# Splitting weights with an accumulating DMA, and value parts side by side in banded attention

## The chip, the cores and the metric

One core of a Trainium2 chip runs the whole program. The metric is device time in microseconds (us) for one execution; lower is better. TensorE (PE) multiplies, VectorE (DVE), ScalarE (ACT) and GpSimd (POOL) do the elementwise work, SyncE (SP) and POOL issue DMAs.

## The reference

A two-layer decoder for 512 tokens, model width 1024, all in float32. Layer 0 is differential attention (8 heads, each with two 64-wide score parts and a 128-wide value) and a SwiGLU FFN of hidden width 2816. Layer 1 is banded attention (16 query heads, 4 key/value heads, head width 64, a window of 128 tokens, one learned sink per head) and another FFN.

```python
def diff_attention(...):                       # per block of 128 queries
    s = einsum('bqhcd,bkhcd->bhcqk', qblk, k) * scale
    p = softmax(where(causal, s, NEG_INF))
    a = p[:, :, 0] - lam * p[:, :, 1]
    o = rms_norm(einsum('bhqk,bkhe->bqhe', a, v), subln) * (1.0 - lambda_init)
    return o.reshape(B, S, DA_V) @ w_o

def swa_sink_attention(...):                   # keys: own block and the one before
    e = exp(s - m)
    p = e / (sum(e) + exp(sink - m))
    o = einsum('bnhgqk,bnkhd->bnqhgd', p, vw)
    return o.reshape(B, S, SW_HEADS * HEAD_DIM) @ w_o
```

## The kernel before

**Numbers in two parts.** PE multiplies in a rounded float32 format. To keep float32 accuracy each operand x is held as hi, x rounded by a cast on ACT, and lo = x - hi, made by a subtract on DVE. A product is three matmuls into one PSUM tile, hi·hi, hi·lo and lo·hi (`mm3`, L291 to L294).

**Weights.** `load_w` (L283) loads one unit (128 partitions x 1024 floats, 512 KB) with a DMA on SP into a tile tagged `raw`, of which two exist (`RAWB`), and `parts` (L262) splits it in two halves h = 0 and 1 of 128x512: the cast of L268, the subtract of L269. The tags `hi` and `lo` have 8 buffers each (`HLB`), four units. Where a norm's gain goes into the weights (L271 to L277, q/k/v of the banded layer) the cast and the subtract take the gain as a factor. `qk_units` loads four units and `v_units` two per pair of heads of the differential attention; `o_units` (L448) loads four for half of an output projection, for rows j = 0, 2 and column halves n = 0, 1, in the order (0,0), (0,1), (2,0), (2,1). `o_block` (L453) then goes, for one block of 128 tokens, through n = 0 with j = 0 to 3 and through n = 1 with j = 0 to 3, each j a `mm3`. The FFN's own splitter (L583 to L587) already has a `move` form: ACT writes the negated rounded value into lo, a DMA issued by POOL adds raw to it in place, and ACT casts hi.

**Stages.** In time: differential attention to about 270 us, its FFN to 600, banded attention to about 785, its FFN to the end. The differential attention runs its four pairs of heads one after the other; the q/k/v products of the next pair, and for the last pair the output projection `o_da`, fill PE between the steps of the current one. `o_da(0, ..)` covers the first two pairs (rows 0 to 511 of the output weights), `o_da(1, ..)` the last two; its first token block runs at 244 to 252 us.

**Banded attention.** It has 16 work units, one per key/value head and query block. Each takes `score` (PE scores, DVE mask and maximum, ACT exponential at L1399 and scaling by the reciprocal sum at L1406), `turn_p` (PE transposes the weights at L1418, ACT and DVE split them into ph and pl of 128x512, four heads of 128 queries side by side) once per key block, and `weigh` (L1424). Query block 0 has one key block, the others two. `weigh` forms the output of four heads in a 128x256 PSUM tile `po`, one buffer: heads 0 and 2 of a group on partitions 0 to 63 and heads 1 and 3 on 64 to 127. For that it keeps v in `vpad`, 64 columns of v with zeros on either side, and shifts the window by 64 columns for e = 0 and 1: two e, three matmuls of 128x256 each, per key block. `split_evac` then reads `po` twice, the cast to `oh` on ACT and the subtract to `ol` on DVE.

**Order.** PE's order is the order of the program text: the tables `DA_STEPS`, `DA_STEPS3`, `SW_AT` give each step a slot, and `Fill` puts so much of the filling products between two slots. DVE, ACT, POOL and SP are ordered by the framework's scheduler, by priorities (`boost` for weight splitting, `evac`, `HOT`). Each engine runs its list in order and waits where an operand or a buffer isn't ready.

## Time and profile before

| | us |
|---|---|
| timed runs | 1122.22, 1124.5, 1125.8 (median 1124.5) |
| profiled execution, span | 1121.8 |
| PE busy | 1101.6 (98%) |
| DVE busy | 1008.4 (90%) |
| ACT busy | 711.3 (63%) |
| POOL busy | 55.5 (5%) |
| median from issue to landing, accumulating DMA of 256 KB | 3.8 |

The profile is one execution, taken by the hardware profiler. Each row of its views has a line of the kernel, an engine, the operation, and output<-inputs by the program's names. What an engine is busy is not what it costs: a wait counts where it holds up work on the engine that sets the end. The time of a profiled execution is its span; the timed runs are separate executions.

### The profile page before, as it was taken

The page shows a single profiled execution, that of the slowest core. Times are in us where ns is not written, and L with a number is a line of the kernel's source. Part 1 is how long each engine was busy: PE and PEld are TensorE (multiplying, and loading weights), DVE is VectorE, ACT ScalarE, POOL GpSimd, SP SyncE. Part 2 cuts the span into 40 slices and gives each one's busy share as a digit, 9 for nine tenths or more (in the row PEclk, how much of TensorE's full clock was granted, in tenths as well). Part 3 has the DMA queues.
Part 4 walks back from the last instruction along what each step waited for, and adds up shares of the span by engine and source line. Part 5 has one row for each costly group of instructions (what it writes and reads, how often), then busy time and mean ns, then how long its engine had stood idle before and what let it go on. Part 6 is the DMA issues. An engine that isn't in the chain of part 4 may idle for free.

```text
span 1121.8 us, 20162 instructions
## 1 busy us (share of the span) xinstructions
PE 1101.6 (98%) x7206; PEld 978.3 (87%) x7206; DVE 1008.4 (90%) x2418; ACT 711.3 (63%) x1577; POOL 55.5 (5%) x76
## 2 busy tenths in 40 slices
PE   8999999999999999999999999999999999999998
PEld 6878888778989989989998778878989989998997
DVE  5979798979999899999998787988899999899997
ACT  6575756454555665675678499697555666566574
POOL 1100000000000010010003000000010000000000
PEclk9999999999999999999999999999999999999999
DMA  6312121124453434336124311120545247246213
GB/s 198 113 57 77 38 77 50 65 72 140 146 162 98 141 80 160 112 82 203 57 48 106 111 41 57 39 76 25 198 138 168 76 104 207 85 104 178 77 30 103
DMA packets 94085, 114.90 MB, mean 102 GB/s; under 512 B 5993, under 2 KB 70914, under 8 KB 93986
## 3 DMA queue, kind: packets, MB, share of 16 engines
q1 hardware_dynamic: 87216, 100.97, 28.1%
q0 software_dynamic: 6720, 12.65, 6.3%
q8 instruction: 56, 0.92, 0.3%
q14 instruction: 43, 0.35, 0.1%
q10 hardware_dynamic: 50, 0.01, 0.0%
HBM read 99.98 MB, written 2.10 MB: 91 GB/s over the span
## 4 chain that ended last, share of the span: by engine, by line
PE 77%; DVE 12%; ACT 6%; DMA 2%; issue 1%; SPq 1%; DVEq 0%; ACTq 0%
PE acc L721 16%; PE tr L721 10%; PE tr L809 9%; PE acc L809 8%; PE acc L292 8%; PE acc L294 8%; PE acc L293 8%; PE po L721 2%; PE tr L435 2%; ACT s L1399 2%; DVE hss L385 1%; ACT s L1406 1%; DVE lo L587 1%; DMA r<-in_w_gate_up_dram 1%; PE tr L310 1%
## 5 line engine op out<-in xcount | busy, mean ns | idle before, releaser
L585 ACT CAST hi<-r 128x512 fp32r<-128x512 f32 x160 | 98.9, 620 | 79.5 <-PE acc L721 35.8
L292 PE MATMUL acc<-hi,hTh 128*128 128x512 f32 (+1 forms) x352 | 132.9, 377 | 2.5 <-DVE vl L1022 1.4
L293 PE MATMUL acc<-lo,hTh 128*128 128x512 f32 (+1 forms) x352 | 124.1, 353 | 0.4 <-DVE lo L269 0.4
L294 PE MATMUL acc<-hi,hTl 128*128 128x512 f32 (+1 forms) x352 | 124.2, 353 | 0.1
L585 ACT CAST hi<-g 128x512 fp32r<-128x512 f32 x154 | 94.9, 618 | 40.8 <-PE acc L293 19.2
L587 DVE TENSOR_TENSOR lo<-r,hi 128x512 fp32r<-128x512 f32 x160 | 105.3, 692 | 6.1 <-ACT hi L585 5.8
L585 ACT CAST hi<-raw 128x512 fp32r<-128x512 f32 x108 | 66.9, 621 | 62.5 <-PE tr L721 18.2
L792 ACT CAST ah<-lf 128x256 fp32r<-128x256 f32 x154 | 61.1, 404 | 47.9 <-PE tr L809 16.0
L721 PE MATMUL acc<-hTh,lo 128*128 128x256 f32 x288 | 81.6, 283 | 0.0
L721 PE MATMUL acc<-hTl,hi 128*128 128x256 f32 x288 | 81.5, 283 | 0.0
L721 PE MATMUL acc<-hTh,hi 128*128 128x256 f32 x288 | 81.5, 283 | 0.0
L721 PE MATMUL acc<-tl,hi 128*128 128x256 f32 x288 | 81.2, 282 | 0.0
L721 PE MATMUL acc<-th,hi 128*128 128x256 f32 x288 | 81.1, 282 | 0.0
L721 PE MATMUL acc<-th,lo 128*128 128x256 f32 x288 | 81.1, 282 | 0.0
L268 ACT CAST hi<-raw 128x512 fp32r<-128x512 f32 x96 | 57.3, 619 | 33.9 <-PE acc L294 24.6
L292 PEld LDWEIGHTS acc<-hi,hTh 128*128 128x128 f32 x352 | 66.7, 190 | 13.4 <-issue 2.6
L587 DVE TENSOR_TENSOR lo<-g,hi 128x512 fp32r<-128x512 f32 x110 | 76.1, 692 | 1.5 <-ACT hi L585 1.4
L294 PEld LDWEIGHTS acc<-hi,hTl 128*128 128x128 f32 x352 | 66.5, 189 | 10.1 <-DVE hTl L907 0.7
L584 POOL DMA_DIRECT2D lo<-g x44 | 38.5, 976 | 716.4 <-ACT lo L583 372.3
L587 DVE TENSOR_TENSOR lo<-raw,hi 128x512 fp32r<-128x512 f32 x108 | 73.4, 692 | 0.0
L269 DVE TENSOR_TENSOR lo<-raw,hi 128x512 fp32r<-128x512 f32 x96 | 64.7, 688 | 9.4 <-ACT hi L268 8.9
L293 PEld LDWEIGHTS acc<-lo,hTh 128*128 128x128 f32 x352 | 66.9, 190 | 6.5 <-DVE lo L269 0.7
(280 smaller groups left out, 3644.7 us busy)
## 6 DMA issues: line engine op xcount, KB each, us to landing
r<-in_w_gate_up_dram SPq DMA_DIRECT2D x80, 512.0 KB, 5.0
g<-in_w_down_dram SPq DMA_DIRECT2D x88, 256.0 KB, 5.4
lo<-g POOLq DMA_DIRECT2D x44, 256.0 KB, 3.8
raw<-in_da_w_qkv_dram SPq DMA_DIRECT2D x30, 256.0 KB, 3.3
raw<-in_da_w_qkv_dram SPq DMA_DIRECT2D x8, 512.0 KB, 3.7
raw<-in_da_w_o_dram SPq DMA_DIRECT2D x8, 512.0 KB, 3.7
raw<-in_w_gate_up_dram SPq DMA_DIRECT2D x8, 512.0 KB, 3.7
raw<-in_sw_w_o_dram SPq DMA_DIRECT2D x8, 512.0 KB, 3.8
```

What stands on the lines that cost most here:

```text
L268: nc.scalar.copy(hi, part)
L269: nc.vector.tensor_tensor(lo, part, hi.bitcast(F32), op=ALU.subtract)
L292: nc.tensor.matmul(dst, sh, mh, start=start, stop=False)
L293: nc.tensor.matmul(dst, sh, ml, start=False, stop=False)
L294: nc.tensor.matmul(dst, sl, mh, start=False, stop=stop)
L435: nc.tensor.matmul(banks[c][:, cols], q[a][rows], k[b][rows], start=a + b == 0, stop=a == 1)
L584: nc.gpsimd.dma_start(out=lo.bitcast(F32), in_=src, accum_op=ALU.add)
L585: nc.scalar.copy(hi, src)
L587: nc.vector.tensor_tensor(lo, src, hi.bitcast(F32), op=ALU.subtract)
L721: nc.tensor.matmul(dst, l[:, k, :], r[:, k, :], start=fresh and k == 0 and i == 0, stop=k == 3 and i == 2, skip_group_check=not fresh)
L792: nc.scalar.copy(ah, src)
L809: nc.tensor.matmul(bank, l[:, tk], r, start=fresh and i == 0 and n == 0, stop=i == len(qs) - 1 and n == 2, skip_group_check=not fresh)
```

## The change

**Moved halves.** `parts` gets a form `move` for the second half (h = 1) of unscaled weights: ACT writes lo = -raw (rounded), a DMA issued by POOL adds raw to it in place, and ACT casts hi. The subtract on DVE goes. Since lo is raw minus raw's rounded value, the numbers are the same. It is used in `qk_units` of pairs 1 to 3 (12 halves), `v_units` of pairs 1 to 3 (6), and the two `o_units` of each attention (16): 34 halves. POOL's list grows from 73 to 107 rows. Pair 0's v, its hand-written first units, the banded layer's scaled q/k/v weights and the FFN's weights are split as before.

**Value parts side by side.** `vpad` and its zeroing go. `vv` holds vh and vl of one head as 128 adjacent columns. Per key block `weigh` now has two matmuls of 128x512, [vh|vl] with ph and with pl, so partitions 0 to 63 of `po` get vh·(ph+pl) and 64 to 127 vl·(ph+pl), for all four heads. ACT copies the lower half of `po` to `ocor` (64x512), DVE adds the halves in two adds of 64x256 into `osum` in SBUF, one of them onto partitions 64 to 127, and `split_evac` splits `osum`. PE has 56 matmuls there in place of 168.

```diff
@@ -259,12 +259,16 @@
             hi, lo = self.halves[i // self.n]
             return hi[:, i % self.n, :], lo[:, i % self.n, :]
 
-    def parts(unit, raw, h, gains=None, by_cols=False):
+    def parts(unit, raw, h, gains=None, by_cols=False, move=False):
         a, b = raw.shape[1:]
         part = raw[:, :, h * b // 2:(h + 1) * b // 2] if by_cols else raw[:, h * a // 2:(h + 1) * a // 2, :]
         hi = wp.tile(list(part.shape), F32R, name=nm("hi"), tag="hi", bufs=HLB)
         lo = wp.tile(list(part.shape), F32R, name=nm("lo"), tag="lo", bufs=HLB)
-        if gains is None:
+        if move:
+            nc.scalar.activation(lo, part, AF.Copy, scale=-1.0)
+            nc.gpsimd.dma_start(out=lo.bitcast(F32), in_=part, accum_op=ALU.add)
+            nc.scalar.copy(hi, part)
+        elif gains is None:
             nc.scalar.copy(hi, part)
             nc.vector.tensor_tensor(lo, part, hi.bitcast(F32), op=ALU.subtract)
         else:
@@ -277,7 +281,7 @@
                                                    op0=ALU.mult, op1=ALU.subtract)
         unit.halves.append((hi, lo))
 
-    def load_w(srcs, a, b, gains=None, by_cols=False):
+    def load_w(srcs, a, b, gains=None, by_cols=False, moved=()):
         unit = Split(a, b, by_cols)
         with tc.high_priority(offset=pri["boost"]):
             raw = wp.tile([P, a, b], F32, name=nm("raw"), tag="raw", bufs=RAWB)
@@ -285,7 +289,7 @@
             for i, src in enumerate(srcs):
                 nc.sync.dma_start(out=raw[:, :, i * w:(i + 1) * w], in_=src)
             for h in range(2):
-                parts(unit, raw, h, gains, by_cols)
+                parts(unit, raw, h, gains, by_cols, h in moved)
         return unit
 
     def mm3(dst, sh, sl, mh, ml, start, stop):
@@ -447,7 +451,7 @@
 
     def o_units(w, k0):
         wv = w.rearrange("(k p) n -> p k n", p=P)
-        return {(j, n): load_w([wv[:, k0 + j:k0 + j + 2, n * 512:(n + 1) * 512]], 2, 512)
+        return {(j, n): load_w([wv[:, k0 + j:k0 + j + 2, n * 512:(n + 1) * 512]], 2, 512, moved=(1,))
                 for j in (0, 2) for n in range(2)}
 
     def o_block(units, pieces, t, ready=None):
@@ -996,11 +1000,12 @@
         def qk_units(self):
             units = []
             for k in range(0, KT, 2):
-                units.append(load_w([wq3[:, k:k + 2, s, self.cs] for s in range(2)], 2, 512))
+                units.append(load_w([wq3[:, k:k + 2, s, self.cs] for s in range(2)], 2, 512, moved=(1,)))
             return units
 
         def v_units(self):
-            return [load_w([wq3[:, k:k + 4, 2, self.cs]], 4, 256) for k in range(0, KT, 4)]
+            moved = (1,) if self.p else ()
+            return [load_w([wq3[:, k:k + 4, 2, self.cs]], 4, 256, moved=moved) for k in range(0, KT, 4)]
 
         def qk_post(self, pts):
             self.ts = copy_out(self.ap, pts, 512)
@@ -1278,7 +1283,7 @@
         ap.tile([P, D], F32, name="s", tag="s", bufs=4)
         ap.tile([P, 512], F32, name="t", tag="t", bufs=4)
         maskS = maskD[:, 256:512]
-        vpad = [ap.tile([P, NT, 9, HD], F32R, name=nm("vpad"), tag=f"vpad{e}") for e in range(2)]
+        vv = ap.tile([P, NT, 4, 2, HD], F32R, name=nm("vv"), tag="vv")
         kT = new_kT(ap, "kTs")
         wqv = sw_w_q[0].rearrange("(k p) n -> p k n", p=P)
         wkv = w_kv.rearrange("(k p) n -> p k n", p=P)
@@ -1290,8 +1295,6 @@
             nc.gpsimd.dma_start(out=gsw[:, 1, :], in_=k_norm.partition_broadcast(P))
             nc.gpsimd.affine_select(out=maskS[:, 0:P], in_=maskS[:, 0:P], pattern=[[1, P]],
                                     compare_op=ALU.is_gt, fill=NEG, base=0, channel_multiplier=-1)
-            for e in range(2):
-                nc.gpsimd.memset(vpad[e][:, :, 0::2, :].bitcast(F32), 0.0)
             tables(Cs, Ss, gsw, HD, nc.gpsimd, nc.gpsimd)
 
         def units_of(*parts):
@@ -1337,10 +1340,10 @@
                     nc.scalar.copy(tt, pts[t][:, 0:256])
                 ts["B"].append(tt)
                 src = heads(pts[t][:, 256:512])
-                dh = vpad[0][:, t, 1::2, :]
+                dh = vv[:, t, :, 0, :]
                 with tc.high_priority(offset=HOT):
                     nc.scalar.activation(dh, src, AF.Copy, scale=rx[:, t:t + 1])
-                    nc.vector.scalar_tensor_tensor(vpad[1][:, t, 1::2, :], src, rx[:, t:t + 1], dh.bitcast(F32),
+                    nc.vector.scalar_tensor_tensor(vv[:, t, :, 1, :], src, rx[:, t:t + 1], dh.bitcast(F32),
                                                    op0=ALU.mult, op1=ALU.subtract)
             vdone.add(0)
             scl["B"] = head_stats(ap, ts["B"], 4)
@@ -1427,15 +1430,19 @@
             po = att("po")
             assert vdone
             for b, blk in enumerate(blocks):
-                for e in range(2):
-                    c0 = (2 * kv + 1 - e) * HD
-                    vf = [vpad[z][:, blk].rearrange("p a e -> p (a e)")[:, c0:c0 + P] for z in range(2)]
-                    es = slice(e * 256, (e + 1) * 256)
-                    mm3(po[:, 0:256], vf[0], vf[1], pT[u, b][0][:, es], pT[u, b][1][:, es],
-                        b == 0 and e == 0, b == nb - 1 and e == 1)
+                v = vv[:, blk, kv].rearrange("p z e -> p (z e)")
+                for z in range(2):
+                    nc.tensor.matmul(po, v, pT[u, b][z], start=b == 0 and z == 0, stop=b == nb - 1 and z == 1)
             oh = ap.tile([P, 2, P], F32R, name=nm("oh"), tag="oh", bufs=OSW)
             ol = ap.tile([P, 2, P], F32R, name=nm("ol"), tag="ol", bufs=OSW)
-            split_evac(oh, ol, po[:, 0:256].rearrange("p (h q) -> p h q", q=P))
+            osum = ap.tile([P, 256], F32, name=nm("osum"), tag="osum", bufs=2)
+            ocor = ap.tile([P, 512], F32, name=nm("ocor"), tag="ocor", bufs=2)
+            with tc.high_priority(offset=pri["evac"]):
+                nc.scalar.copy(ocor[0:HD, :], po[HD:P, :])
+                for e in range(2):
+                    es = slice(e * 256, (e + 1) * 256)
+                    nc.vector.tensor_tensor(osum[e * HD:(e + 1) * HD, :], po[0:HD, es], ocor[0:HD, es], op=ALU.add)
+            split_evac(oh, ol, osum.rearrange("p (h q) -> p h q", q=P))
             o_all[kv, i] = (oh, ol)
 
         def pieces_sw(ch):
```

**Where the order moves: ACT at the end of the differential attention.** ACT's list near the last two units of the output projection's second half; before (raw_659 is unit (0,1), raw_664 is (2,0), raw_669 is (2,1), aT are the transposed weights of the last pair, osb its evacuated output):

```order
L268 CAST hi_665_3197<-raw_664_3195 128x512
L268 CAST hi_667_3201<-raw_664_3195 128x512
L298 CAST aT_644_3102<-tr_647_3105 128x128
L298 CAST aT_635_3076<-tr_650_3130 128x2x128
L298 CAST aT_644_3102<-tr_649_3118 128x2x128
L298 CAST aT_636_3077<-tr_650_3130 128x2x128
L1121 COPY osb_652_3170<-po_651_3145 128x512
L1123 ACTIVATE osq_653_3172<-osb_652_3170 128x512
L268 CAST hi_670_3207<-raw_669_3205 128x512
L268 CAST hi_672_3211<-raw_669_3205 128x512
```

And of the changed kernel, from the last aT on, with the line numbers of its own text (L268 is the negating cast, L270 the hi cast of a moved half, L272 that of an unmoved one; raw_659, raw_664 and raw_669 are the same units):

```order
L302 CAST aT_636_3099<-tr_650_3152 128x2x128
L272 CAST hi_665_3221<-raw_664_3219 128x512
L270 CAST hi_667_3225<-raw_664_3219 128x512
L268 ACTIVATE lo_663_3215<-raw_659_3208 128x512
L268 ACTIVATE lo_668_3226<-raw_664_3219 128x512
L1126 COPY osb_652_3192<-po_651_3167 128x512
L1128 ACTIVATE osq_653_3194<-osb_652_3192 128x512
L272 CAST hi_670_3232<-raw_669_3230 128x512
L270 CAST hi_672_3236<-raw_669_3230 128x512
L268 ACTIVATE lo_673_3237<-raw_669_3230 128x512
L526 ACTIVATE xn_689_3331,fss_688_3330<-xs_76 128x1024
```

Both casts of (2,0) have moved behind the last aT; the negating casts of (0,1) and (2,0) come after them, and that of (2,1) after both of its hi casts.

**ACT in the middle of the banded attention.** From a split of the weights (ph) to the scaling by the reciprocal sum of the next work unit; s_1856 before and s_1871 after are the same unit's weights. Before:

```order
L298 CAST ph_1867_9344<-tr_1866_9339 128x512
L268 CAST hi_1896_9449<-raw_1893_9443 128x512
L1399 ACTIVATE s_1856_9285,sm_1860_9305<-s_1856_9285,mx_1857_9286,hscl_1758_8875 128x256 x4
L1401 ACTIVATE es_1861_9308<-es_1861_9308 128x4
L298 CAST oh_1878_9397<-po_1877_9390 128x256
L298 CAST q_1883_9410<-tr_1882_9407 128x256
L298 CAST ph_1886_9422<-tr_1885_9417 128x512
L1406 ACTIVATE s_1856_9285<-s_1856_9285,rs_1862_9316 128x256 x4
```

And now (raw_1912 is unit (0,1) of the second output half, raw_1917 is (2,0)):

```order
L302 CAST ph_1884_9356<-tr_1883_9351 128x512
L270 CAST hi_1910_9452<-raw_1907_9446 128x512
L302 CAST oh_1879_9336<-osum_1881_9338 128x256
L272 CAST hi_1913_9459<-raw_1912_9457 128x512
L270 CAST hi_1915_9463<-raw_1912_9457 128x512
L1441 COPY ocor_1898_9408<-po_1894_9402 64x512
L1402 ACTIVATE s_1871_9296,sm_1875_9316<-s_1871_9296,mx_1872_9297,hscl_1767_8891 128x256 x4
L1404 ACTIVATE es_1876_9319<-es_1876_9319 128x4
L302 CAST oh_1895_9405<-osum_1897_9407 128x256
L268 ACTIVATE lo_1916_9464<-raw_1912_9457 128x512
L272 CAST hi_1918_9470<-raw_1917_9468 128x512
L1409 ACTIVATE s_1871_9296<-s_1871_9296,rs_1877_9327 128x256 x4
```

A copy ocor, a negating cast and the first cast of (2,0) now stand ahead of the scaling (L1409), and the q and ph casts have moved behind it.

**PE at one value product.** One work unit with two key blocks, and what follows. Before:

```order
L292 MATMUL po_1961_9707<-ph_1930_9581,vpad_1487_7623 128x256
L293 MATMUL po_1961_9707<-pl_1931_9582,vpad_1487_7623 128x256
L294 MATMUL po_1961_9707<-ph_1930_9581,vpad_1488_7624 128x256
L292 MATMUL po_1961_9707<-ph_1930_9581,vpad_1487_7623 128x256
L293 MATMUL po_1961_9707<-pl_1931_9582,vpad_1487_7623 128x256
L294 MATMUL po_1961_9707<-ph_1930_9581,vpad_1488_7624 128x256
L292 MATMUL po_1961_9707<-ph_1936_9610,vpad_1487_7623 128x256
L293 MATMUL po_1961_9707<-pl_1937_9611,vpad_1487_7623 128x256
L294 MATMUL po_1961_9707<-ph_1936_9610,vpad_1488_7624 128x256
L292 MATMUL po_1961_9707<-ph_1936_9610,vpad_1487_7623 128x256
L293 MATMUL po_1961_9707<-pl_1937_9611,vpad_1487_7623 128x256
L294 MATMUL po_1961_9707<-ph_1936_9610,vpad_1488_7624 128x256
```

And now:

```order
L1435 MATMUL po_1984_9718<-ph_1951_9595,vv_1487_7649 128x512
L1435 MATMUL po_1984_9718<-pl_1952_9596,vv_1487_7649 128x512
L1435 MATMUL po_1984_9718<-ph_1959_9621,vv_1487_7649 128x512
L1435 MATMUL po_1984_9718<-pl_1960_9622,vv_1487_7649 128x512
L1421 MATMUL tr_1989_9732<-ident_80,s_1936_9523 128x128 x4
```

Twelve matmuls of 128x256 have become four of 128x512; the transposes of the next unit's weights follow as before.

## The prediction

> **What bounds the kernel now.** I read the page's totals and chain first, then a table of busy time by stage, then the waits of PE, and last the timelines of the two places where a moved half is wanted soon. The page, its first part and its chain:
>
> ```profile
> span 1121.8 us, 20162 instructions
> PE 1101.6 (98%) x7206; PEld 978.3 (87%) x7206; DVE 1008.4 (90%) x2418; ACT 711.3 (63%) x1577; POOL 55.5 (5%) x76
> PE 77%; DVE 12%; ACT 6%; DMA 2%; issue 1%; SPq 1%; DVEq 0%; ACTq 0%
> ```
>
> PE is the bound on average, but PE runs in an order written out by hand, so what it waits for at one place counts at once. The table by stage (window: length, then busy us and instructions of PE, PEld, DVE, ACT and POOL); the first row is the end of the differential attention, the others are the banded attention:
>
> ```profile
> 212.00:262.00 50.00, 47.52 (x258) 37.92 (x257) 40.26 (x129) 23.74 (x57) 0.29 (x1) 1.00 0.14 43
> 645.00:700.00 55.00, 52.30 (x329) 41.84 (x328) 43.43 (x173) 49.76 (x144) 0.00 (x0) 1.00 0.16 50
> 728.00:760.00 32.00, 31.59 (x207) 25.22 (x206) 26.43 (x97) 29.02 (x81) 0.00 (x0) 1.00 0.22 67
> 760.00:786.00 26.00, 25.00 (x155) 20.81 (x153) 22.87 (x69) 20.61 (x50) 0.00 (x0) 1.00 0.13 37
> ```
>
> ACT, 63% over the span, is at 90% in the first and second banded rows (49.76 of 55, 29.02 of 32). Work added to ACT there isn't free. Both FFN stages run their old code, so I give them 0. PE's waits in the end of the differential attention (us in total, times, longest):
>
> ```profile
> PE po L1140 <- DVE ro L249: 1.3, 2, 1.0
> PE tr L1100 <- DVE s L1084: 1.2, 1, 1.2
> PE tr L435 <- DVE qkT L445: 0.8, 1, 0.8
> ```
>
> That is 3.3 us in 70, the most that a relieved DVE could give back there.
>
> **The moved halves, instruction by instruction.** The FFN already makes some of its halves in this way, so each price has a row: the negating cast, one such cast with its DMA (ACT and POOL timelines), the DMA's time from issue to landing (min/median/max, from the view of its line), and the page's medians for the loads.
>
> ```profile
> L583 ACT ACTIVATE lo<-g x44: 615/626/632, 301.6 to 1104.7; 128x512 fp32r<-128x512 f32 x44
> 301.60 0.62 ACT L583 ACTIVATE lo<-g 128x512 fp32r<-128x512 f32 x1
> 302.52 0.94 POOL L584 DMA_DIRECT2D lo<-g  x1 [69.62 <-ACT lo L583]
> DMA to landing us min/median/max: 3.2/3.8/8.6
> raw<-in_da_w_o_dram SPq DMA_DIRECT2D x8, 512.0 KB, 3.7
> raw<-in_sw_w_o_dram SPq DMA_DIRECT2D x8, 512.0 KB, 3.8
> ```
>
> From the end of the negating cast to the DMA is 302.52 - 302.22 = 0.3 us, and 3.8 to landing. So a moved half has its lo 0.62 + 0.3 + 3.8 = 4.7 us after ACT starts on it. The old way takes a cast and a subtract, 1.3 us when both engines are free:
>
> ```profile
> 239.43 1.14 ACT L268 CAST hi<-raw 128x512 fp32r<-128x512 f32 x2
> 243.55 1.29 DVE L269 TENSOR_TENSOR lo<-raw,hi 128x512 fp32r<-128x512 f32 x2
> ```
>
> Two casts take 1.14, so one more costs ACT 0.52; a subtract less saves DVE 0.60. For 34 halves that is 17.7 us onto ACT and 20.4 off DVE, spread over two stages. The DMA also reads raw, so the raw buffer is given back about 4 us later, and only two exist: the later load is the second price.
>
> The Trainium skill ("DMA: Bandwidth & Descriptors", section "Anatomy of one DMA — SWDGE (gpsimd) path") fits a GpSimd-issued DMA as 2.0 us plus bytes over 436e3 per us; for 256 KB it would be an estimated 2.6 us, below even the 3.2 of the quickest of the 44 here. By that figure each accumulate would land 1.2 us sooner and the two in a row below would cost 2.4 us less; the measured row decides.
>
> **Differential attention, the 18 q/k/v halves: 0.** The tightest is the first (second half of the first unit, DVE timeline) and its first use (PE timeline):
>
> ```profile
> 40.22 0.69 DVE L269 TENSOR_TENSOR lo<-raw,hi 128x512 fp32r<-128x512 f32 x1
> 51.07 0.39 PE L293 MATMUL acc<-lo,hTh 128*128 128x512 f32 x1
> ```
>
> It is ready at 40.9 and wanted at 51.1. Ten us cover a lag grown by 3.4 and a load put off by 4. Without that cover each would cost up to 3.4 us. ACT has room here too, with 23.74 busy of 50 at the end. What DVE's relief gives: the waits on qkT and s end behind DVE work that can only start when ACT's exponentials or PE's scores are there, so I take 1.0 us of the 3.3 (range 0 to 2.8, the rest being the next term's).
>
> **The last four output units: +7.6 - 0.4.** This is the largest term. Call them (rows, columns) in load order: (0,0), (0,1), (2,0), (2,1). The first and third share one raw buffer, the second and fourth the other. ACT, SP and PE timelines of before:
>
> ```profile
> 242.74 0.37 ACT L298 CAST aT<-tr 128x256 fp32r<-128x256 f32 x1 [1.46 <-DVE aT L299]
> 247.04 1.14 ACT L268 CAST hi<-raw 128x512 fp32r<-128x512 f32 x2 [1.22 <-DMA raw<-in_da_w_o_dram]
> 234.58 9.15 SPq L286 DMA_DIRECT2D raw<-in_da_w_o_dram  x2
> 246.65 0.39 PE L293 MATMUL acc<-lo,oh 128*128 128x512 f32 x1
> 250.32 0.39 PE L293 MATMUL acc<-lo,oh 128*128 128x512 f32 x1
> 252.67 0.62 PE L1140 MATMUL po<-ident,ro 128*128 128x128 f32 x4 [0.37 <-DVE ro L249]
> 264.47 0.62 ACT L268 CAST hi<-raw 128x512 fp32r<-128x512 f32 x1
> ```
>
> Before, (2,1) is loaded the moment (0,1) has been split (second SP issue, about 243.4), arrives at 247.04, and its last lo is there at 249.66, 0.66 us before PE wants it at 250.32. There is no cover for a 4.7 us lag, and there are now two accumulates and a load in a row. In the new order ACT casts both halves of (2,0) after the last aT (242.7 to 243.1; I take 242.7), and only then negates for (0,1): two casts 1.04, so it starts at 243.75 and ends at 244.4. Its DMA is issued at 244.7 and lands at 248.5. Only now is the raw buffer free: (2,1) is issued and arrives 3.7 later, at 252.2. Two hi casts, 1.04, stand ahead of its negating cast (253.25 to 253.85); + 0.3 + 3.8 makes 257.95. PE wants it at 250.32: 7.6 us late. On the way the lo of (2,0) lands at 249.0 against 246.65; those 2.4 are part of the 7.6. POOL has nothing else to do there (0.29 busy in the window), so no queue is added. What is queued behind: on PE the rest of the token block, then the other blocks and the FFN; on ACT the normalised rows of the FFN, which need PE's result anyway; on SP the first FFN loads, which can then go out at 258 at the latest and land by 262, while their first cast stood at 264.47 (last row) and is itself put off with PE: 0. Since PE stands still, the 0.4 us for ro (row above) goes. Bounds: both accumulates at 3.2 and the aT 0.4 earlier give 6.0; one of them at the maximum of 8.6 gives 12.4. I take the medians, as the window's DMA share is only 0.14.
>
> **Banded attention, value product: -7.4 of PE, not all kept.** Line of the old product with its count, the pitches of both shapes (PE timelines, starts of following rows), what PE waits for before turning the weights, and two such groups of four:
>
> ```profile
> L292 PE MATMUL po<-ph,vpad x56: 277/283/387, 666.1 to 777.0; 128*128 128x256 f32 x56
> 776.35 0.28 PE L293 MATMUL po<-pl,vpad 128*128 128x256 f32 x1
> 776.47 0.28 PE L294 MATMUL po<-ph,vpad 128*128 128x256 f32 x1
> 250.55 0.39 PE L294 MATMUL acc<-hi,ol 128*128 128x512 f32 x1
>   ACT s L1406: 2.4, 9
> 749.34 1.52 PE L1418 MATMUL tr<-ident,s 128*128 128x128 f32 x4
> 774.41 0.60 PE L1418 MATMUL tr<-ident,s 128*128 128x128 f32 x4
> ```
>
> A 256-wide matmul follows after 0.12, a 512-wide one after 0.23 (250.32 to 250.55). 168 x 0.12 = 20.2 become 56 x 0.227 = 12.7, or 7.4 less: 0.53 for each of the 12 units of two blocks, 0.27 for the other four. But already PE takes 1.52 instead of 0.60 for four transposes, standing for ACT's scaling of the weights, nine times in the stage. And ACT gets more: a copy of half of po for 16 units, nearest row the 0.59 us osb copy (pitch 0.5), 7.8 us; and 8 x 0.52 = 4.2 for the moved halves. DVE gets 32 adds of 64x256 at the 0.42 (pitch 0.33) of
>
> ```profile
> L299 DVE TENSOR_TENSOR ol<-po,oh x16: 392/416/425, 670.7 to 778.6; 128x256 fp32r<-128x256 f32 x16
> 244.57 0.59 ACT L1121 COPY osb<-po 128x512 f32<-128x512 f32 x1 [1.46 <-PE po L294]
> ```
>
> so 10.6 - 8 x 0.6 = +5.8. Where the lock is tight, ACT's order from the first cast of the second output half on, old times:
>
> ```profile
> 732.41 0.61 ACT L268 CAST hi<-raw 128x512 fp32r<-128x512 f32 x1
> 733.01 1.71 ACT L1406 ACTIVATE s<-s,rs 128x256 f32<-128x256 f32 x4
> 740.36 1.72 ACT L1406 ACTIVATE s<-s,rs 128x256 f32<-128x256 f32 x4
> 748.78 1.71 ACT L1406 ACTIVATE s<-s,rs 128x256 f32<-128x256 f32 x4 [0.16 <-DVE rs L1404]
> ```
>
> New: cast, scaling, copy, negate ends at 735.65; lands 739.75; raw of (2,0) at 743.5; its cast stands ahead of the next scaling, which starts at 744.1, not 740.36: +3.7. The one after has behind it two casts, a negate and a copy, and starts near 752.4, not 748.78: +3.6. From there five units of 0.53 give 2.6 back on PE, and the longer road from po to ol (copy 0.5 and two adds 0.75 ahead of it, as I add them) costs about 0.5 at the last units, where po has one buffer. Before 728 PE's gain goes into ACT's and DVE's queues. Net +1.5; bounds: -5 if ACT overtakes (its idle 3 of 32 and 5 of 26 us), +5 if nothing is given back.
>
> **Sum.** -1.0 + 7.6 - 0.4 + 1.5 = +7.7: a span of 1129.5. The profiled execution spans 1121.8, 2.7 under the median of 1124.5, so 1132.2 as timed; I say 1132.
>
> **Rivals.** (1) *The gain arrives*: lo halves land in time, since ACT's scheduled position is reached earlier than I work out, and PE keeps 5 of its 7.4 and 1.4 from DVE: 1118. For it: DVE is at 90% and PE at 98%. Against: the 0.66 us of slack at 250.32. It decides if (2,1) is loaded before 246. (2) *They cancel*: accumulates at 3.2, +6.0 - 1.4 at the first place, -4 in the banded one: about 1125. For it the quiet DMA window, against it the ACT lock. (3) *ACT falls further behind*: one accumulate near 7 instead of 3.8, so +11 - 1.4, and +5 in the banded stage: 1139. For it the 8.6 maximum, against it that those stand in the FFN. Slower either way, but a separate size.
>
> **Chances.** Forecast 0.53, (3) 0.12, (2) 0.17, (1) 0.18. A measurement of this kernel tells about 0.3%, 3.4 us, from no change. Slower by more: 0.65; within: 0.17; faster: 0.18. The forecast's own range is 1128 to 1137; for 8 in 10 it must reach towards (2) and part of (1), so 1121 to 1138.
>
> **What would show it.** In the new trace: PE waiting in the second column half of the first token block of the last output units for a DMA on lo, some 5 us or more, and the load of (2,1) issued near 248; no wait on q/k/v parts; transposes of weights in the banded stage each some 3.5 us later at 750, and less later at 785. Wrong: if the load of (2,1) comes early, if PE's waits on ACT shrink, or if DVE's relief gives over 3 us before 230.

## The result and the profile after

| | before | after |
|---|---|---|
| timed runs, median (us) | 1124.45 (1122.22 to 1125.8, 4 runs) | 1165.03 (1163.24 to 1166.87, 4 runs) |
| profiled span (us) | 1121.8 | 1164.4 |

The changed kernel is slower: ratio 1.0368, 95% interval 1.0349 to 1.0387, or 40.6 us. The forecast was slower by 7.7, range 1121 to 1138; the side was right, the size far off and the range too narrow.

The header and the busy times of the page after:

```profile
span 1164.4 us, 20122 instructions
PE 1114.3 (96%) x7094; PEld 976.3 (84%) x7094; DVE 1008.6 (87%) x2416; ACT 740.2 (64%) x1627; POOL 83.1 (7%) x108
```

PE has 112 instructions fewer and is busy 12.7 us longer. So not all of the loss is waiting: PE also ran more slowly. In the table by stage (window: length, busy us and count of PE, PEld, DVE, ACT, POOL, then PE's granted clock, DMA share and GB/s) the clock shows where. Three of its rows, one from the differential and two from the banded attention:

```profile
60.00:110.00 50.00, 45.14 (x285) 37.39 (x285) 37.76 (x140) 34.15 (x82) 5.13 (x6) 1.00 0.35 87
728.00:760.00 32.00, 29.42 (x154) 21.30 (x155) 27.48 (x103) 18.95 (x58) 1.13 (x2) 0.89 0.11 34
760.00:786.00 26.00, 21.40 (x103) 14.81 (x103) 15.83 (x53) 23.10 (x60) 3.50 (x4) 0.87 0.48 122
```

Before, the clock was 1.00 in every row of that table. PE's longest waits before in the banded attention (640 to 790 us), and then those after, for the whole span (us, times, longest):

```profile
PE tr L1418 <- DVE mx L1388: 1.4, 1, 1.4
PE tr L1418 <- ACT s L1406: 1.0, 1, 1.0
```

```profile
PE acc L296 <- ACT oh L302: 6.7, 3, 2.8
PE tr L1105 <- DVE s L1089: 5.2, 5, 2.9
PE acc L297 <- DMA lo<-raw: 4.3, 2, 2.3
PE po L1435 <- ACT sq L388: 3.7, 1, 3.7
PE tr L1421 <- ACT s L1409: 3.4, 2, 2.4
PE po L1435 <- DVE osum L1444: 3.0, 2, 2.4
```

To see where the time goes I compared the start of the same PE instruction in two traces: how many us later it starts than before, at the time (of before) at the head of the column. The FFN between 285 and 600 adds no loss; over it the lag even falls by 1.1 us.

```
at us        46    66    90   243   260   285   599   690   720   750   790
after      -0.4  +3.9  +5.7  +6.4 +14.4 +15.7 +14.6 +16.7 +23.9 +31.8 +43.8
```

Three losses: about 6 us between 46 and 90 us (pair 0's softmax; forecast 0, or a gain), 9.3 between 243 and 285 (forecast 7.2), and 29 in the banded attention, 600 to 790 of before (forecast 1.5).

**First loss.** ACT's timeline after, the exponential that followed in the trace before, and PE's row after:

```profile
58.73 0.62 ACT L272 CAST hi<-raw 128x512 fp32r<-128x512 f32 x1 [3.00 <-DMA raw<-in_da_w_qkv_dram]
61.18 0.49 ACT L1081 ACTIVATE s<-s,mx,hscl 128x128 f32<-128x128 f32 x1
64.35 0.33 PE L1105 MATMUL tr<-ident,s 128*128 128x128 f32 x1 [2.87 <-DVE s L1089]
```

```profile
57.13 0.50 ACT L1076 ACTIVATE s<-s,mx,hscl 128x128 f32<-128x128 f32 x1
```

ACT takes its list in order. A hi cast of pair 1's v weights, whose product comes more than 20 us later, waits 3.0 us for its load; the load went out at 55.1, when the accumulate issued at 51.75 had landed and given the raw buffer back. Behind the cast stand the first exponentials of the score, which PE wants at once. They start at 61.18, not 57.13.

In PE's lag this is one step of three: 2.5 us at 53, where PE waits for the cast qkT, which stands behind two hi casts that had waited 1.5 and 1.4 us for their loads; 3.1 at 61; and 1.9 more up to 90. There is also a gain that the table's columns hide. Before, PE waited at 46 us for the low part of v:

```profile
PE acc L292 <- DVE vl L1022: 1.4, 1, 1.4
```

After, this wait is gone: ACT makes v's high part at 44.63 and not at 46.17, where two weight casts stood ahead of it. So the changed kernel is 1.8 ahead at 47 us, and loses 7.5 from there to 90.

**Second loss.** The forecast's chain came as written. SP (loads of the last two output units), ACT (negating casts, then the wait for (2,1)), POOL and PE after:

```profile
244.71 9.52 SPq L290 DMA_DIRECT2D raw<-in_da_w_o_dram  x2
249.28 1.15 ACT L268 ACTIVATE lo<-raw 128x512 fp32r<-128x512 f32 x2
257.41 0.62 ACT L272 CAST hi<-raw 128x512 fp32r<-128x512 f32 x1 [5.24 <-DMA raw<-in_da_w_o_dram]
258.46 0.62 ACT L268 ACTIVATE lo<-raw 128x512 fp32r<-128x512 f32 x1
259.38 0.85 POOL L269 DMA_DIRECT2D lo<-raw  x1 [7.43 <-DVE rsq_t L248]
255.14 0.50 PE L297 MATMUL acc<-lo,oh 128*128 128x512 f32 x1 [1.94 <-DMA lo<-raw]
259.31 0.50 PE L297 MATMUL acc<-lo,oh 128*128 128x512 f32 x1 [0.72 <-DVE lo L273]
262.63 0.79 PE L297 MATMUL acc<-lo,oh 128*128 128x512 f32 x1 [2.35 <-DMA lo<-raw]
```

Second load issued at 253.9, arrived 257.4, negated, accumulated 259.38, landed at about 262.6. Over the 34 halves the accumulates were a little quicker than the FFN's 3.8 (min/median/max); the two in this chain took 3.5 and 3.2, the one of (2,0) 4.3:

```profile
DMA to landing us min/median/max: 3.2/3.3/5.7
```

So PE waits 1.9 + 0.7 + 2.4 = 5.0, not 7.6. But then it runs at half clock (third number from the end):

```profile
263.00:265.00 2.00, 2.00 (x6) 1.52 (x6) 0.69 (x1) 0.39 (x1) 0.00 (x0) 0.50 0.56 139
265.00:267.00 2.00, 2.00 (x9) 1.60 (x7) 0.00 (x0) 0.76 (x2) 0.00 (x0) 0.50 0.35 123
267.00:269.00 2.00, 2.00 (x9) 1.64 (x8) 1.45 (x6) 0.62 (x1) 0.00 (x0) 0.73 0.00 0
```

4 us at 0.50 and 2 at 0.73 are 2.5 us of PE work lost. 5.0 and 2.5 make 7.5 of the 8.0 between 243 and 260.

**Third loss.** One instance in the banded attention after: ACT's copy of po, its cast to oh, and the PE matmul that needs it.

```profile
786.51 0.58 ACT L1441 COPY ocor<-po 64x512 f32<-64x512 f32 x1
788.37 0.39 ACT L302 CAST oh<-osum 128x256 fp32r<-128x256 f32 x1
788.81 0.50 PE L296 MATMUL acc<-hi,oh 128*128 128x512 f32 x1 [2.75 <-ACT oh L302]
```

Waits are not all of it. From 600 us to the end of the banded attention PE's waits add up to 24.9 us (4.8 before), and the granted clock is 0.50 for 27 us of that stretch (never before), which loses 12.9 us of PE's work. For example, behind the wait just shown:

```profile
791.00:793.00 2.00, 2.00 (x15) 1.65 (x15) 1.43 (x3) 0.00 (x0) 0.00 (x0) 0.50 0.00 0
```

Where the waits come from, the runs below take apart.

### The profile page after: what moved, and what is told of

Read it like the earlier page. It is cut to its first block, busy times and chain, and to the rows that moved or that the text cites. A ratio compares the mean times of both kernels' runs of the same rounds, so it can differ in the third digit from the quotient of the medians.

```text
span 1164.4 us, 20122 instructions
## 1 busy us (share of the span) xinstructions
PE 1114.3 (96%) x7094; PEld 976.3 (84%) x7094; DVE 1008.6 (87%) x2416; ACT 740.2 (64%) x1627; POOL 83.1 (7%) x108
## 3 DMA queue, kind: packets, MB, share of 16 engines
q0 software_dynamic: 11616, 21.57, 10.2%
## 4 chain that ended last, share of the span: by engine, by line
PE 64%; ACT 6%; DVE 5%; issue 1%; DMA 1%; DVEq 0%; ACTq 0%; SPq 0%; POOLq 0%
PE acc L725 18%; PE tr L725 11%; PE tr L813 9%; PE acc L813 8%; PE acc L298 4%; PE acc L297 4%; PE acc L296 4%; PE po L725 2%; ACT s L1402 2%; ACT s L1409 1%; PE po L813 1%; PE tr L314 1%; PE tr L1421 1%; DMA lo<-raw 1%; ACT ph L302 1%
## 5 line engine op out<-in xcount | busy, mean ns | idle before, releaser
L589 ACT CAST hi<-raw 128x512 fp32r<-128x512 f32 x108 | 67.0, 621 | 62.5 <-PE tr L725 19.8
L298 PEld LDWEIGHTS acc<-hi,hTl 128*128 128x128 f32 x352 | 66.5, 189 | 10.6 <-DVE hTl L911 0.7
L591 DVE TENSOR_TENSOR lo<-raw,hi 128x512 fp32r<-128x512 f32 x108 | 72.6, 685 | 0.0
L296 PE MATMUL acc<-hi,oh 128*128 128x512 f32 x128 | 58.2, 455 | 6.7 <-ACT oh L302 6.7
L297 PE MATMUL acc<-hTl,hi 128*128 128x256 f32 (+1 forms) x192 | 61.3, 319 | 1.2 <-DVE hTl L303 1.2
```

The source lines that it names most:

```text
L296: nc.tensor.matmul(dst, sh, mh, start=start, stop=False)
L297: nc.tensor.matmul(dst, sh, ml, start=False, stop=False)
L298: nc.tensor.matmul(dst, sl, mh, start=False, stop=stop)
L589: nc.scalar.copy(hi, src)
L591: nc.vector.tensor_tensor(lo, src, hi.bitcast(F32), op=ALU.subtract)
```

## The experiments

Times are medians, each against the runs of the kernel before on the same chip.

### Each part alone

All moves, old value product: `weigh`, `vpad` and their zeroing as before.

> All 34 moved halves, with the old value product on zero-padded v. In the changed kernel's trace PE falls 7.6 us behind between 50 and 90 us, 9 more at the end of the differential attention and 29 more in the banded attention. Theory V (the banded loss comes from the longer way from po to ol in the new value product): 16 us for the differential attention plus at most 5 in the banded one, +16 to +21, about 1143. Theory M (the banded loss comes from the moved output halves and the ACT time they take): +16 plus 20 or more, 1160 or above.

1145.72 against 1123.35, ratio 1.0201 (1.0185 to 1.0216), +22.4.

The value product alone (the diff shows the changed words only):

```diff
-moved=(1,)          # in o_units, qk_units
+moved=()
-            moved = (1,) if self.p else ()
+            moved = ()
```

> The new value product alone, no moved half. Theory V: PE waits for oh, osum and ph as in the changed kernel, +20 or more, about 1145 to 1150. Theory M: PE keeps part of the 7.4 us of matmuls saved, -5 to +3, about 1120 to 1128.

1148.47 against 1123.35, ratio 1.0221 (1.0204 to 1.0238), +25.1. Theory V comes nearest: the value product with 112 matmuls fewer is the largest loss in the banded stage. But the moves cost more there than V allowed, so M is not nothing.

The q, k, v halves alone, and the differential attention's output halves alone:

> Only the 18 moved halves of the q, k and v weights of pairs 1 to 3. Theory of the blocked list (a hi cast that waits for a later raw load stands in ACT's list ahead of the first exponentials): +5 to +7, about 1130, and the PE loss stands at 50 to 90 us. The prediction's 0, or a gain of 1 us from DVE: 1123 to 1125.

1129.59 against 1123.35, ratio 1.0062 (1.0043 to 1.0081), +6.2.

> Only the 8 moved halves of the differential attention's output weights. Theory of the late lo (two accumulates and one load in a row ahead of the last unit): +7 to +9, about 1132 to 1133, nearly all between 244 and 260 us. If instead the q/k/v moves had pushed these units late: under +3.

1131.82 against 1123.35, ratio 1.0073 (1.0058 to 1.0088), +8.5.

> Only the 8 moved halves of the banded attention's output weights. If the parts add, +22.4 (all moves) - 6.2 (q, k, v) - 8.5 (first output weights) leaves +7 to +8. The prediction had, for these alone, the scalings of two work units 3.6 us later and some given back: +1 to +4.

1132.08 against 1123.91, ratio 1.0066 (1.0043 to 1.0089), +8.2. The three sets of moved halves make 6.2 + 8.5 + 8.2 = 22.9, all moves +22.4: they add. All moves and the value product would make 47.5; together they cost 40.6, so the two overlap by 7 (by 5 in the banded stage of the traces: 8.6 and 25.5 alone, 29.2 together). In the traces, in us behind the kernel before, as above:

```
at us          46    66    90   243   260   285   599   690   720   750   790
moves        +0.3  +4.1  +5.6  +6.3 +13.6 +14.9 +13.8 +13.8 +15.3 +22.7 +22.4
qkv          +0.7  +5.2  +6.2  +6.9  +7.0  +6.9  +5.8  +5.8  +5.8  +5.8  +5.8
o_da         +0.2  +0.4  +0.5  +0.7  +7.6  +8.9  +7.8  +7.8  +7.8  +7.8  +7.8
o_sw         +0.1  +0.1  +0.1  +0.0  +0.0  -0.1  -1.0  -1.0  +0.5  +6.3  +6.0
value        -0.0  +0.3  +0.3  +0.2  +0.3  +0.9  -0.2  +2.1  +8.3 +14.9 +25.3
```

Each set of halves loses in one stretch; the value product loses all along the banded stage. In the differential attention it is the place where a load or a lo is late. The banded output halves lose between 742 and 746. ACT's timeline of that run:

```profile
743.73 0.62 ACT L272 CAST hi<-raw 128x512 fp32r<-128x512 f32 x1 [0.97 <-DMA raw<-in_sw_w_o_dram]
746.15 0.57 ACT L302 CAST ph<-tr 128x512 fp32r<-128x512 f32 x1
752.11 1.71 ACT L1411 ACTIVATE s<-s,rs 128x256 f32<-128x256 f32 x4 [0.15 <-DVE rs L1409]
```

The forecast had 743.5 for this cast and 752.4 for this scaling. (The scaling that it had at 744.1 stands ahead of the cast in this run, at 740.55; in the changed kernel, 25.2 us behind at that place, it stands at 769.11, as forecast.) What it didn't have is who else stands behind the cast: the split (ph) of already transposed weights. Before, the same split was done at 739.88, ahead of these casts:

```profile
739.88 0.59 ACT L298 CAST ph<-tr 128x512 fp32r<-128x512 f32 x1
```

PE's longest wait of that run between 700 and 800:

```profile
PE po L296 <- ACT ph L302: 2.9, 1, 2.9
```

Of the 6.3 us by which the split is later, the load's wait is 0.97. The rest is the new order of ACT's list, with a scaling, two negating casts, three hi casts and an exponential now ahead of it. So here the late load is the smaller part.

### Is the late load the price?

```diff
-RAWB = 2
+RAWB = 3
```

on all moves, and on the kernel before as the control.

> All 34 moved halves with the old value product, and a third raw buffer, so that the next load need not wait for the accumulating DMA. Theory that the late load is the price (ACT's list blocked by a cast that waits for it, and the last output unit loaded 5 us late): of the +22.4 at least 12 go, total +3 to +10. If the accumulating DMA's own lag is the price: +18 or more.

> The kernel before with a third raw buffer, as the control: the load of the last output units comes earlier, which nothing waits for. -1 to +1; if the earlier loads shift ACT's list, up to 5 either way.

All moves with three raw buffers 1150.56, ratio 1.0234 (1.0217 to 1.025), +26.7; the kernel before with three 1136.06, ratio 1.0109 (1.0091 to 1.0127), +12.2, both against 1123.91. A third buffer costs 12 us without any moved half, outside what was expected of the control: 5.3 before 46 us and 6.7 between 260 and 285. Less the control, all moves cost 14.5 of their 22.4, which neither theory had. So only the difference of the two, stage by stage, can be read, with the reservation that both run 4 us later than the kernel before when the weights of pair 1 are split:

```
at us          46    66    90   243   260   285   599   690   720   750   790
before_raw3  +5.3  +4.2  +4.2  +4.2  +3.7 +10.4  +9.4  +9.3  +9.3 +10.5 +11.5
moves_raw3   +5.6  +4.5  +4.8  +5.5  +7.0 +14.1 +13.0 +13.0 +15.6 +21.6 +26.9
```

Until 243 the moves now cost 1.3, not 6; at 243 to 260 they cost 2.0, not 7.3. ACT's longest waits between 28 and 110 us, of the q, k, v run and of all moves with three buffers:

```profile
ACT hi L272 <- DMA raw<-in_da_w_qkv_dram: 9.4, 4, 3.7
```

```profile
ACT hi L272 <- PE acc L298: 6.8, 6, 1.9
```

The waits of ACT for raw are gone, and with them most of the loss. In the differential attention the price is the late load more than the accumulate's own lag. In the banded stage the third buffer doesn't help (11.7 more than the control): that part isn't shown to be the load.

> Moved halves only in the q, k and v weights of pairs 2 and 3 (12 halves), old value product. If the +6.2 is the one place where a cast waiting for its load stands ahead of the first exponentials (pair 1's weights, 50 to 65 us): -1 to +1.5. If every moved half costs its ACT time or its lag: +3 to +4. A gain of 1 us from DVE, as the prediction had: -1.

Against the q, k, v run (ends of two lines of the code, and a whole one):

```diff
-2, 512, moved=(1,)))
+2, 512, moved=(1,) if self.p > 1 else ()))
-            moved = (1,) if self.p else ()
+            moved = (1,) if self.p > 1 else ()
```

1124.06 against 1123.13, ratio 1.0005 (0.9996 to 1.0014): no change. Twelve of the 18 halves are free within about 1 us, the six of pair 1 cost nearly all of the 6.2. And DVE's relief is worth nothing here.

### Why does the value product lose?

Its matmuls without the sum of the two halves, so that the output lacks it (the seven lines with `osum`, `ocor`, the copy and the two adds go too):

```diff
-            split_evac(oh, ol, osum.rearrange("p (h q) -> p h q", q=P))
+            split_evac(oh, ol, po[:, 0:256].rearrange("p (h q) -> p h q", q=P))
```

> The new value product, but oh and ol are split from the first 256 columns of po as before: the two halves of po are not added, the output leaves that sum out. If the matmuls alone are worth what their pitches say and PE is the bound: -4 to -7, about 1117 to 1120. If ACT's softmax keeps PE locked whatever PE saves: -2 to +1. If the loss of 25 us came from the product's shape: +15 or more.

1127.68 against 1123.92, ratio 1.0038 (1.0026 to 1.005), +3.8. The matmuls saved are worth nothing by themselves: PE was 1.4 us ahead at 730 us and 2.9 behind at 790. The sum costs the other 21. In the run of the value product (PE, then ACT, then DVE timelines) one unit's last value matmul, the copy and adds that free `po`, and the next unit's first:

```profile
705.13 0.50 PE L1435 MATMUL po<-pl,vv 128*128 128x512 f32 x1
713.57 0.77 PE L1435 MATMUL po<-ph,vv 128*128 128x512 f32 x1 [4.03 <-DVE osum L1444]
709.18 1.17 ACT L388 ACTIVATE sq<-t 128x512 f32<-128x512 f32 x2
710.23 1.71 ACT L1409 ACTIVATE s<-s,rs 128x256 f32<-128x256 f32 x4
711.96 0.58 ACT L1441 COPY ocor<-po 64x512 f32<-64x512 f32 x1
712.58 0.85 DVE L1444 TENSOR_TENSOR osum<-po,ocor 64x256 f32<-64x256 f32 x2 [1.30 <-ACT ocor L1441]
```

`po` is complete at 705.6; the copy, 0.58 long, starts at 711.96, behind exponentials, a cast, squares and a scaling. The one buffer is free 7.8 us after it was full, 6.3 of them in front of the copy. This is the longest of the 16; over all of them the median from a full `po` to a free one is 3.2 us (2.2 before), and to a finished ol 5.0 (2.2 before). PE's longest waits of that run between 600 and 815:

```profile
PE po L1435 <- DVE osum L1444: 7.0, 3, 4.0
PE acc L296 <- ACT oh L302: 6.8, 3, 2.8
```

Is it the place in the list? The copy, adds and split at a higher priority (the diff shows the copy and adds; the split to oh and ol gets the same line):

```diff
-            with tc.high_priority(offset=pri["evac"]):
+            with tc.high_priority(offset=HOT):
```

> The new value product with the copy, the adds and the split to oh and ol at the priority HOT, so that they stand ahead of exponentials and norms in the lists of ACT and DVE. Theory of the list position: the waits of PE on osum and oh (14 us in the run of the value product alone) shrink below 4, total +0 to +8. Theory of the chain's length (copy, two adds, cast, subtract take their 2 us wherever they stand, on a PE order that gave 0.8): +15 or more.

1146.86 against 1123.92, ratio 1.0204 (1.0184 to 1.0224), +22.9. The waits on osum and oh fell from 13.8 to 3.6, as the list theory had it, but the time did not:

```profile
PE tr L1421 <- ACT s L1409: 6.5, 6, 2.6
PE po L1435 <- ACT ph L302: 4.2, 1, 4.2
```

The work that the copy went ahead of, the scaling and the split of the weights, is late in its place. So the theory of the copy's own place falls. The time is what was written for the chain's length (+15 or more), but not for its reason: `po` is free 2.0 us after it is full (median, before 2.2), ol is done after 3.3, and PE hardly waits there. What the copy gains, other work of ACT loses.

> The new value product with the copy of po's lower half on DVE in place of ACT: one change of engine fewer, 8 us less on ACT, 5 more on DVE. If ACT's load or list is what makes osum late: +5 to +12. If it's the length of the chain: +20 to +25, as DVE now makes three steps one after the other. If DVE is as full as ACT: +25 or more.

```diff
-                nc.scalar.copy(ocor[0:HD, :], po[HD:P, :])
+                nc.vector.tensor_copy(ocor[0:HD, :], po[HD:P, :])
```

1140.86 against 1123.92, ratio 1.0152 (1.0135 to 1.017), +16.9, between what ACT's load and the chain's length would each have given. 8 us of the 25 come with ACT doing the copy. In the traces the larger part of them is PE's clock, which stands at half for 17 us of the banded stage in the run of the value product and for 3.4 here. One stretch of each, the value product's first:

```profile
700.00:728.00 28.00, 22.98 (x113) 16.77 (x112) 24.68 (x79) 17.53 (x42) 1.14 (x2) 0.88 0.18 57
```

```profile
700.00:728.00 28.00, 23.20 (x128) 17.79 (x130) 27.59 (x88) 18.10 (x49) 1.14 (x2) 1.00 0.18 57
```

> The kernel before with its old value product, but po is first copied to SBUF by ACT (128x256, 0.35 us) and oh and ol are split from the copy: one step more between po and oh, and 5 us more on ACT. Chain length or ACT load: +4 to +10. If the one buffer of po is what counts, it is released earlier than before (after one copy, not after a cast and a subtract): -2 to +2.

> The kernel before, plus one ACT copy of 128x256 from oh for each of the 16 work units, which nothing reads: the same ACT work as the hop (+10.6), but behind oh and not ahead of it. If ACT's time is the price: +6 to +11. If the length of the way from po to oh is: -1 to +3.

```diff
+                nc.scalar.copy(ocor, po[:, 0:256])       # hop: before the split, which then reads ocor
+                nc.scalar.copy(ocor, oh ...)             # load: after the split, read by nothing
```

The hop: 1134.53 against 1123.92, ratio 1.0097 (1.0073 to 1.012), +10.6. The same copies behind oh: 1130.07 against 1123.91, ratio 1.0052 (1.0035 to 1.0068), +6.2 (in its profiled execution 2.1 of them stand before 60 us, where nothing was edited). Sixteen short copies add about 6 us to ACT's busy time, and cost as much or more in time, ahead of the chain 4 us more than behind it. The single buffer of `po` is not what holds PE in the hop: it is free after 2.0 us (median), before after 2.2.

Does PE merely ask too early? Output products allowed only 2.5 slots after the last `weigh` (one line of the edit):

```diff
+        todo += [(SW_AT[5 * u + 4] + 2.5, u, mark) for u in range(16)]
```

> The new value product alone, with PE's order changed: the output products of a token block may be taken only from 2.5 slots (about 2.5 us) after the last weigh they need. If the +25 comes from PE's hand-written order, which asks for oh and ol sooner than the longer chain gives them: +8 to +18. If ACT's time and list set it wherever PE asks: +22 to +28.

1151.39 against 1123.13, ratio 1.0244 (1.0226 to 1.0262), +28.3. The waits on oh fell from 6.8 to 1.4, and others took their place, above all

```profile
PE tr L439 <- DVE pl L303: 5.3, 1, 5.3
```

PE's order is not the cause by itself.

And what does a re-sorted list cost with no work added?

```diff
-SW_EVAC = 30
+SW_EVAC = 33
```

> The kernel before with the evacuation priority of the banded stage at 33 in place of 30: no work is added, taken away or made longer, only the lists of ACT (65 lines of difference) and DVE (131) are sorted otherwise. If a re-sorted list alone costs what the runs with little added work cost (+4 to +11): +3 or more. If added work or a longer chain is needed for a loss: -2 to +2.

1129.56 against 1123.13, ratio 1.0047 (1.0028 to 1.0066), +6.4 (its profiled execution spans 1125.0, +3.2). With the value product without its sum:

> The value product without the sum of its halves (the output leaves that sum out), with the lists sorted by the other priority. If PE's 7.4 us were lost only by an unlucky sorting of the lists: another sorting gives another time, perhaps -3 to +1. If ACT's softmax holds PE whatever it saves: +2 to +5 again.

1133.51 against 1123.13, ratio 1.0084 (1.0063 to 1.0106), +10.4. So merely another order of the same ACT and DVE work cost 6.4 us here, and 6.6 on the product without its sum. The +3.8 of that product and the +6.2 of the unread copies are of that size and can't be read as the price of matmuls or a copy; the +8.2 of the banded output halves and the +10.6 of the hop are not far above it. A lucky order in which the matmuls saved come out as time wasn't found by the one other order tried.

How PE loses the time in these runs, from 600 us to the end of the banded attention of each profiled execution (waits over 0.15 us; PE's busy time at clock 0.50, halved):

```
us                   before  evac33  nosum  nosum_evac33  value  value_hot  value_dve  after
PE's waits              4.8     9.4   12.4          15.3   24.6       22.6       19.9   24.9
lost to half clock      0.0     0.0    0.0           8.0    7.9        9.5        1.7   12.9
```

Where the clock falls, a few us of waiting more can become 10 us of time. That is most of what parts the two sortings of the product without its sum, and the larger part of what parts value_dve from value.

No run beat the kernel before; the moves of pairs 2 and 3 alone equal it.

## Why the prediction was wrong

**What bounds.** Right that PE's waits at single places count, and that ACT in the banded attention is near full. But 98% on PE and nearly no waits were read as a stage with some room on either side. The run with SW_EVAC at 33 speaks against it: the one other sorting of the lists that was tried lost 6.4 us (3.2 in its profiled execution). The forecast had no term for a schedule that is sorted anew, and none for PE's clock. The lock to ACT was also read too strongly: the row "ACT s L1406: 2.4, 9" counts nine gaps of the weight loads between 726 and 780, in three places; PE itself waited for the scaling once in the stage, 1.0 us.

**The 18 q/k/v halves: 0, wrong by 6.** The step that failed is "Ten us cover a lag grown by 3.4 and a load put off by 4". The lag and the load were right, and lo was in time. The cover was looked for at the user of lo; the late load also holds up the engine that casts it, and everything behind that cast in its list: the exponentials stand 4 us later (57.13 to 61.18). The run with moves in pairs 2 and 3 alone (+0.9, within noise) and the third buffer bear this out. What is queued behind the wait was worked out for the last output units and not for this term.

**DVE's relief, -1.0.** Nothing: the run with pairs 2 and 3 moved takes 12 subtracts off DVE (busy 1008.4 to 1004.1 us) and isn't faster. The one gain, the 1.4 us at vl, came from a new order of ACT's list.

**The last output units, +7.6 - 0.4: the right size, 8.0 in the trace at 243 to 260, 8.5 timed alone, but partly by luck.** The chain was as worked out, with the load of (2,1) behind the accumulate of (0,1): issue forecast for 248.5 plus PE's lag of 6.4, or 254.9, seen 253.9. In parts it was off both ways, and the errors cancel: the accumulates of the chain took 3.5 and 3.2 and not 3.8 each, waits 5.0 and not 7.6, and the halved clock added 2.5 that was in no term. A further 1.3 came in waits on hTl (the low part of the FFN's transposed input) at 285 to 287 of the changed kernel.
The estimate of 2.6 us by the fit in the Trainium skill ("DMA: Bandwidth & Descriptors", section "Anatomy of one DMA — SWDGE (gpsimd) path") was too low for these accumulates: the quickest took 3.2.

**The banded attention, +1.5 within -5 and +5: 29.** Two steps failed. For the moved output halves the times of the cast and of the scalings were met to 0.3 us (in that run, or 25.2 us behind in the changed kernel), but the split of ph behind the same cast had no term; it kept PE waiting 2.9, and the moves cost 8.2 there. For the value product the step is "the longer road from po to ol [...] costs about 0.5 at the last units". The road was added up as bare durations, 1.25. In the trace its median grew by 2.8 us (2.2 to 5.0) and its longest from 4.7 to 8.9, because its steps wait their turn in the lists of ACT and DVE, and there are three more of them than before. PE's waits grew from 4.8 to 24.6, and half clock took another 7.9. The sum costs 21 us over the version without it. The bound of 5 came from "nothing is given back"; it had no case in which PE waits at unit after unit, and none in which its clock falls.

**What the runs leave open.** Of the 21 us of the sum, 8 go with the copy on ACT in place of DVE. How these and the rest divide between the length of the chain, ACT's and DVE's added time, the lists' new order and the clock isn't settled, since every such edit also sorts the lists anew. Whether PE's order, fitted by hand to the old product, could be fitted to the new one was not tried beyond one shift (+28.3).

**Rivals.** The one that the slow side goes further, (3), was nearest, but for another reason: no accumulate of the 34 came near 7 us. Those with a gain or no change fell with the waits on raw and on osum.

## What to carry to other kernels

A transfer that keeps an input buffer longer delays the next load, and on an engine that takes its list in order the cast waiting for that load stops all behind it; look at who stands behind the cast, not only at who needs its result. Fewer instructions on the engine at 98% gained nothing here, since they added turns through the lists of the others: 112 matmuls fewer, with the sum that they need, cost 25 us. In a stage whose order was fitted by hand, measure a null edit that only re-sorts (here +6.4) before a difference of a few us is put down to the edit. And look at PE's granted clock beside its waits: 12.9 of the 29 us in the banded attention were work at half clock.

## What the runs showed of the hardware

After a wait of 4.0 us in the run of the value product, PE's granted clock stood at half for over 5 us. A 128x512 matmul there follows the one before after 0.43 us, and after 0.23 at full clock (table by time, the clock is the third number from the end):

```profile
709.00:713.60 4.60, 0.57 (x4) 0.17 (x2) 2.92 (x7) 4.58 (x11) 0.00 (x0) 0.90 0.36 123
713.60:716.00 2.40, 2.03 (x4) 1.01 (x5) 2.40 (x6) 0.88 (x2) 0.00 (x0) 0.50 0.00 0
716.00:719.00 3.00, 3.00 (x8) 2.04 (x9) 2.94 (x13) 1.17 (x3) 0.60 (x1) 0.50 0.15 44
```

The Trainium skill ("TensorE: Matmul & The Clock Gate", section "Why this matters for your kernels") warns of idle gaps above about 3 us between bursts. The 4.0 us gap agrees with it, but the traces show that shorter gaps aren't safe, and they decide here.

A wait of 2.9 us at 61 in the changed kernel and one of 2.8 at 769 in the value run left the clock at 1.00. One of 2.75 at 786 in the changed kernel was followed by 0.50, and so were two of 1.7 and 2.0 at 247 and 255 in the run with the differential attention's output halves alone, where waits of 3.7 and a clock loss of 3.4 make up the 6.9 us lost. Over the 18 traces, behind their first 20 us, the clock fell during or within 3.5 us after all 12 waits above 3 us, 7 of 9 between 2.5 and 3, 15 of 29 between 1.7 and 2.5, and 6 of 77 between 1.0 and 1.7. Ahead of the last 5 us of each run, every stretch at half clock lasted 3.4, 6.8 or 10.2 us. So a term for the clock belongs into a sum whose waits reach about 2 us.
